# Dense products of a two-block float32 network: one matmul with plain float32 operands in place of three float32r passes

## The chip, the cores and the metric

The kernel runs on one core of a Trainium2 chip. The metric is the device time of one execution in microseconds (us). PE is the matrix engine (TensorE); a matmul holds one operand still in the array (the weights in PE's sense, loaded by LDWEIGHTS, here called PEld) and streams the columns of the other through it. DVE (VectorE), ACT (ScalarE) and POOL (GpSimd) work on elements; SP issues the transfers (DMA) from the chip's memory.

## What is computed

The input is x, 256 tokens of 1024 float32 features. Three parts follow one another; the dense products in them are what this case is about.

```python
# first block
p = rmsnorm(x) @ w_in                      # [256,1024] @ [1024,9248]
y_rnn = rglru_branch(...) @ w_rnn_proj     # [256,1536] @ [1536,1024]
y_dn = deltanet_branch(...) @ w_dn_proj    # [256,1024] @ [1024,1024]
x = x + (g_rnn * y_rnn + g_dn * y_dn) @ w_out
x = x + (silu(gt) * up) @ w_down           # gt, up = split(rmsnorm(x) @ w_gate_up)
# then two layers of: four attention-like branches from one wide projection,
# their gated sum through a projection, a layer norm, and a mixture of 16384 experts:
# a = gelu(x @ u.T); out = (gates * a) @ v   # u, v: [16384, 1024]
```

The program computes the expert part densely: the activations of all 16384 experts, times gates that are zero for those not chosen, times `v`. Everything is float32 from end to end.

## The kernel before

**Operands.** Every dense product is done in float32r, a form of float32 with fewer bits. To keep the accuracy of float32, each operand is cut into two float32r parts, `hi` (the value rounded) and `lo` (what is left), and a product is three passes into the same PSUM tile: hi x hi, lo x hi, hi x lo.

- `split_w` (L84) streams one block of weights, 128 rows of up to 1024 words (512 KB): SP issues the load of `wraw` (L91), ACT casts it to `whi` (L98; DVE in turns set by `share`), DVE subtracts and writes `wlo` (L100; POOL for two blocks). `wraw`, `whi` and `wlo` have three buffers each. `hold` can tie a block's two steps to come after given instructions, to keep them out of a norm's way.
- `split_x` (L108) does the same for an activation in SBUF: ACT writes `hi` (L111), DVE `lo` (L112).
- The normalized activations live as two tiles `xh` and `xl` of [128, 8, 256], written by `norm_evac` (L225) from PSUM: affine steps on ACT (L233) and DVE (L232), a copy for `hi` (L244), a subtraction for `lo` (L247).

**Products with stationary weights.** `lin_s` (L124) makes 128 output features for all 256 tokens from one block of weights of eight chunks: the 128x128 pieces of the block stand in the array and x^T streams, 256 columns at a time. For each chunk there is a pass with `whi` (L137) and one with `wlo` (L138) against `xh`, and after them eight passes of `whi` against `xl` (L140): 24 passes a block, into one bank `st` of two that alternate. Its `evac` takes the result out of PSUM.

**Products with moving weights.** `lin_m` (L144) keeps a 128x128 piece of x^T and streams the weights, 512 columns at a time, into four PSUM banks (two halves of the tokens, two of the columns). Per block these are four groups of three passes:

```python
mm(o, xh[:, kc, s], hi[:, c], start=first and n == 0, stop=False)   # L155
mm(o, xh[:, kc, s], lo[:, c], start=False, stop=False)              # L156
mm(o, xl[:, kc, s], hi[:, c], start=False, stop=last and n == len(steps) - 1)  # L157
```

In `mixers` the helper `project` does its products of 256 columns with `mm3` (L114, passes at L116 to L118).

**Order.** `block1` (L706), `mixers` (L1346) and `peer` (L1636) write out the order by hand. Chains of small work on DVE and ACT (a delta rule, a recurrence, attention, the routing of experts) are woven with blocks of `lin_s` by lists of calls (`units`, `weave`, `Fill`), so that PE always has a block to work on. All loads go through SP's queue in the order of the program, and a load waits there until its buffer is free.

`peer` is the longest part, and runs twice. Its 128 blocks of `u` go through `lin_s`: 50 of them (`X1`) while the routing runs, the others between 32 groups of `gates` (L1674), which build the gates of eight tokens with 16 products of f16 operands each (L1684, L1685). Then 128 blocks of `v` go through `lin_m`; for each the activations of 128 experts, `W[e // H][:, e % H]`, are split (`split`, L1657) one step ahead.

**Plain float32.** Many small products are plain float32 already: the normalizing transposes of `norm_T` (L222), the sums with alpha x in `add_alpha_x` (L78; it first adds `xh` and `xl` on DVE, L75), the recurrence's gates (L675), the delta rule's matrices (L473, L547, L636), the experts' keys (L1536).

Of the kernel before, what the change touches and what calls it, by code (L numbers as in the profile page):

```python
# [10 lines left out]
F32R = mybir.dt.float32r  # L11
# [9 lines left out]
P = 128  # L21
T = 256
# [5 lines left out]
ALPHA = 4.0 ** 0.25  # L28


class K:
    """Shared state of the program under construction and its small building blocks."""

    def __init__(self, ctx, tc, A):
        self.tc, self.nc, self.A = tc, tc.nc, A
        self.ctx = ctx
        E = ctx.enter_context
        self.cp = E(tc.tile_pool(name="cp", bufs=1))
        self.wp = E(tc.tile_pool(name="wp", bufs=4))
# [3 lines left out]
        self.held = []  # L43
        self.share(0)
# [35 lines left out]
    def share(self, *turns):  # L80
        """Engines of the first parts of the next weights: 1 for DVE, 0 for ACT, in turns."""
        self.turns = cycle(turns)

    def split_w(self, src, words, eng=None):  # L84
        """Stream one unit of weights and split it exactly into two float32r parts."""
        nc = self.nc
        self.hi_dve = next(self.turns)
        raw = self.t(self.wp, [P, 1024], "wraw", bufs=3)
        hi = self.t(self.wp, [P, 1024], "whi", F32R, bufs=3)
        lo = self.t(self.wp, [P, 1024], "wlo", F32R, bufs=3)  # L90
        nc.sync.dma_start(raw[:, :words], src)  # L91
        h = self.held.pop(0) if self.held else None
        after = lambda i: self.tc.issue_after(h[i].ins) if h and h[i] else nullcontext()
        with after(0):
            if self.hi_dve:
                nc.vector.tensor_copy(hi[:, :words], raw[:, :words])
            else:
                nc.scalar.copy(hi[:, :words], raw[:, :words])  # L98
        with after(1):
            (eng or nc.vector).tensor_sub(lo[:, :words], raw[:, :words], hi[:, :words].bitcast(F32))  # L100
        return hi, lo

    def hold(self, *after):
        """Keep the next splits of weights but the first out of the way of a norm: their two parts come after the given
        instructions."""
        self.held = [None, *after]

    def split_x(self, hi, lo, src):  # L108
        """hi + lo = src exactly; src in SBUF."""
        nc = self.nc  # L110
        nc.scalar.copy(hi, src)  # L111
        return nc.vector.tensor_sub(lo, src, hi.bitcast(F32))  # L112

    def mm3(self, out, lh, ll, rh, rl, start, stop):  # L114
        mm = self.nc.tensor.matmul
        mm(out, lh, rh, start=start, stop=False)  # L116
        mm(out, lh, rl, start=False, stop=False)
        mm(out, ll, rh, start=False, stop=stop)  # L118

    def units(self, x, src, evac, n, eng=None):  # L120
        """The products of lin_s as a list of calls."""
        return [lambda j=j: self.lin_s(x, src[j:j + 1], lambda _, o: evac(j, o), n=1, eng=eng) for j in range(n)]

    def lin_s(self, x, src, evac, kcs=(KC,), n=None, eng=None):  # L124
        """out^T tiles of 128 columns: weights stationary, x^T moving. src [units, 128, words]."""
        xh, xl = x
        u = 0
        for j in range(n):
            o = self.bank("st")
            c0, ct = 0, sum(kcs)  # L130
            for kc in kcs:
                hi, lo = self.split_w(src[u], kc * P, eng)
                u += 1
                mm = self.nc.tensor.matmul
# [9 lines left out]
    def lin_m(self, acc, steps, ncol, first, last):  # L144
        """token-layout out [t, col] += x^T[kc] w[kc] for steps (x, kc, source of w), by halves of t; acc[half][bank]."""
        ws = [self.split_w(src, ncol) for _, _, src in steps]
        mm = self.nc.tensor.matmul
        for h in range(2):
            s = slice(h * P, (h + 1) * P)
            for b in range((ncol + 511) // 512):  # L150
                c = slice(b * 512, min(ncol, (b + 1) * 512))
                o = acc[h][b][:, :c.stop - c.start]
                for n, ((xh, xl), kc, _) in enumerate(steps):
                    hi, lo = ws[n]
                    mm(o, xh[:, kc, s], hi[:, c], start=first and n == 0, stop=False)  # L155
                    mm(o, xh[:, kc, s], lo[:, c], start=False, stop=False)  # L156
                    mm(o, xl[:, kc, s], hi[:, c], start=False, stop=last and n == len(steps) - 1)  # L157

    def lin_m_all(self, acc, x, src, ncol, count, extra=None):
        """All chunks of a token-layout product, the last two together."""  # L160
# [9 lines left out]
    def rstd(self, out, ss, scale, eps):  # L170
        """out = (ss * scale + eps) ** -0.5 for few columns."""
# [6 lines left out]
    def softplus(self, out, y, pool, sign=1.0):  # L178
        """out = softplus(sign * y), accurate in relative terms, for few columns."""
# [17 lines left out]
    def transposes(self, y, kcs, evac):  # L197
        """PE-transposes of y [128 t, 2, f] (token layout) as a list of calls; evac(c, psum [128, 2, 256])."""
# [11 lines left out]
    def norm_T(self, pool, half, evac):  # L210
        """Transposes of a normalized x: half(h) -> y [128 t, 1024] and a scale [128 t, 1];
        evac(c -> psum [128, 256] of a chunk)."""
        nc = self.nc
        os = None
        for h in range(2):
            y, r = half(h)
            d = self.t(pool, [P, P], "nd", bufs=2)
            self.scaled = nc.vector.tensor_scalar(d, self.ident, r, None, op0=OP.mult)
# [6 lines left out]
    def norm_evac(self, pool, g, b, xx):  # L225
        """Gain, bias and exact split of transposed chunks."""
        nc = self.nc

        def affine(dst, o, c, eng):
            gs, bs = g[:, c:c + 1], b[:, c:c + 1] if b is not None else 0.0  # L230
            if eng:
                return nc.vector.tensor_scalar(dst, o(c), gs, bs, op0=OP.mult, op1=OP.add)  # L232
            return nc.scalar.activation(dst, o(c), AF.Identity, scale=gs, bias=bs)  # L233
# [17 lines left out]
    def rmsnorm_T(self, half, g, pool, xh, xl):  # L251
        """hi/lo of (rmsnorm(x) * g)^T; half(h) -> x [128 t, 1024] of a half, g [128, 8] per feature."""
# [10 lines left out]
        self.norm_T(pool, norm, self.norm_evac(pool, g, None, (xh, xl)))  # L263
# [23 lines left out]
def conv_tile(k, pads, n, o, w, dst, bias=None):  # L287
    """Centred 4-tap depthwise convolution along t of psum o [128, 256]; w [128, 4]."""
# [8 lines left out]
def weave(gen, units, per=1):  # L297
    """Run a generator with calls of a list between its steps."""
# [11 lines left out]
class Fill:  # L310
    """Calls to put where other work waits: fill(n) makes the next n, fill.upto(n) all before the n-th."""
# [26 lines left out]
class DeltaNet:  # L338
    """Gated delta rule of 8 heads in both directions, chunks of 128 tokens."""
# [13 lines left out]
    def project(self):  # L353
        """Keys and queries (unnormalized) and the gates' inputs."""
# [28 lines left out]
    def gates(self):  # L383
# [20 lines left out]
        # in the order (direction, head group, half, head), and its negative  # L404
# [41 lines left out]
    def matrices(self, hg):  # L446
        """Decayed k k^T (without the learning rates) and k q^T of 4 heads; both directions share a tile by triangles."""
# [32 lines left out]
    def small(self):  # L480
        """Inverses of the 32-blocks on the diagonal, scaled by the learning rates of their rows, and their transposes:
# [1316 lines left out]
```

## Time and profile before

| | us |
|---|---|
| median of 3 runs | 3051.55 (3049.89 to 3051.58) |
| span of the profiled execution, first to last instruction | 3042.9 |
| between the two | 8.65 |

The page gives no time of its own for the profiled execution beside its span; the difference to the median is what lies around the span in an execution. A profile lists for each instruction when it began and how long it was busy. For PE the beginnings are recorded and the ends are modelled, so consecutive records overlap in the list, and the distance from one beginning to the next is the time that an instruction really took from the engine. "float32r" and plain float32 operands both show as f32 in PE's rows; the line of the code tells them apart. The chain of waits follows the last instruction back to what released it, step by step.

### The profile page before, as it was taken

The page shows a single profiled execution, that of the slowest core. Times are in us where ns is not written, and L with a number is a line of the kernel's source. Part 1 is how long each engine was busy: PE and PEld are TensorE (multiplying, and loading weights), DVE is VectorE, ACT ScalarE, POOL GpSimd, SP SyncE. Part 2 cuts the span into 40 slices and gives each one's busy share as a digit, 9 for nine tenths or more (in the row PEclk, how much of TensorE's full clock was granted, in tenths as well). Part 3 has the DMA queues.
Part 4 walks back from the last instruction along what each step waited for, and adds up shares of the span by engine and source line. Part 5 has one row for each costly group of instructions (what it writes and reads, how often), then busy time and mean ns, then how long its engine had stood idle before and what let it go on. Part 6 is the DMA issues. An engine that isn't in the chain of part 4 may idle for free.

```text
span 3042.9 us, 50388 instructions
## 1 busy us (share of the span) xinstructions
PE 2977.5 (98%) x19954; PEld 2682.9 (88%) x19954; DVE 1990.7 (65%) x3464; ACT 1457.4 (48%) x2514; POOL 76.9 (3%) x96
## 2 busy tenths in 40 slices
PE   8989999999999999999999999999999999999998
PEld 7888999989999898888888889999989888888887
DVE  7787765565767965566556666576895565656565
ACT  6667644455444543333444446544453333344444
POOL 0012000000000000000000000000000000000000
PEclk9999999999999998888999999999998888899999
DMA  5342456553445443323455555345543323355554
GB/s 196 105 132 87 153 198 193 190 178 120 142 158 188 166 154 111 111 104 113 157 190 191 193 191 203 111 139 184 180 166 133 111 104 111 109 182 194 190 191 159
DMA packets 129742, 470.96 MB, mean 155 GB/s; under 512 B 14785, under 2 KB 15073, under 8 KB 128609
## 3 DMA queue, kind: packets, MB, share of 16 engines
q1 hardware_dynamic: 129504, 467.73, 45.1%
q8 instruction: 157, 2.57, 0.3%
q14 instruction: 81, 0.66, 0.1%
HBM read 466.63 MB, written 1.05 MB: 154 GB/s over the span
## 4 chain that ended last, share of the span: by engine, by line
PE 89%; DVE 6%; ACT 3%; issue 1%; POOL 1%; DMA 0%; SPq 0%; POOLq 0%; DVEq 0%; ACTq 0%
PE st L137 16%; PE st L138 15%; PE st L140 14%; PE acc L155 8%; PE acc L157 8%; PE acc L156 8%; PE bank L1684 4%; PE bank L1685 4%; DVE wlo L100 2%; PE bank L157 1%; PE bank L155 1%; PE bank L156 1%; PE bank L1290 1%; ACT whi L98 0%; PE bank L1536 0%
## 5 line engine op out<-in xcount | busy, mean ns | idle before, releaser
L100 DVE TENSOR_TENSOR wlo<-wraw,whi 128x1024 fp32r<-128x1024 f32 (+2 forms) x859 | 1048.0, 1222 | 424.7 <-ACT whi L98 421.6
L137 PE MATMUL st<-xh,whi 128*128 128x256 f32 x4040 | 1049.1, 297 | 8.4 <-ACT gy L784 2.2
L138 PE MATMUL st<-xh,wlo 128*128 128x256 f32 x4040 | 1022.1, 291 | 18.3 <-DVE wlo L100 18.3
L98 ACT CAST whi<-wraw 128x1024 fp32r<-128x1024 f32 (+2 forms) x852 | 887.2, 1042 | 183.4 <-PE st L140 51.8
L137 PEld LDWEIGHTS st<-xh,whi 128*128 128x128 f32 x4040 | 815.2, 202 | 32.6 <-issue 9.1
L138 PEld LDWEIGHTS st<-xh,wlo 128*128 128x128 f32 x4040 | 813.5, 201 | 26.5 <-DVE wlo L100 22.3
L140 PE MATMUL st<-xl,whi 128*128 128x256 f32 x4040 | 552.4, 280 | 0.2
L140 PEld LDWEIGHTS st<-xl,whi 128*128 128x128 f32 x4040 | 506.8, 190 | 2.0 <-DVE xl L247 1.0
L155 PE MATMUL acc<-whi,wwh 128*128 128x512 f32 x1024 | 404.8, 395 | 0.0
L157 PE MATMUL acc<-whi,wwl 128*128 128x512 f32 x1024 | 401.6, 392 | 0.0
L156 PE MATMUL acc<-wlo,wwh 128*128 128x512 f32 x1024 | 397.7, 388 | 0.0
L111 ACT CAST wwh<-W 128x256 fp32r<-128x256 f32 x256 | 104.0, 407 | 363.6 <-PE acc L156 357.5
L157 PEld LDWEIGHTS acc<-whi,wwl 128*128 128x128 f32 x1024 | 192.3, 188 | 45.0
L156 PEld LDWEIGHTS acc<-wlo,wwh 128*128 128x128 f32 x1024 | 192.3, 188 | 42.4
L155 PEld LDWEIGHTS acc<-whi,wwh 128*128 128x128 f32 x1024 | 192.6, 188 | 37.8
L1684 PE MATMUL bank<-oah,ob 128*128 128x128 f16 x512 | 212.9, 416 | 0.1
L1685 PE MATMUL bank<-oal,ob 128*128 128x128 f16 x512 | 211.4, 413 | 0.0
L112 DVE TENSOR_TENSOR wwl<-W,wwh 128x256 fp32r<-128x256 f32 x256 | 108.6, 425 | 151.9 <-ACT wwh L111 149.7
L1691 DVE SCALAR_TENSOR_TENSOR W<-bank,W 128x512 f32<-128x512 f32 (+26 forms) x114 | 59.4, 557 | 194.2 <-PE bank L1685 194.2
L1702 ACT ACTIVATE ge<-st 128x8 f32<-128x8 f32 (+25 forms) x156 | 44.4, 284 | 291.9 <-PE st L140 291.9
L1694 ACT ACTIVATE W<-bank 128x96 f32<-128x96 f32 (+16 forms) x76 | 29.4, 404 | 203.2 <-DVE W L1691 203.2
L1685 PEld LDWEIGHTS <-ob 128*128 128x128 f16 x512 | 75.9, 148 | 39.5
(518 smaller groups left out, 2957.1 us busy)
## 6 DMA issues: line engine op xcount, KB each, us to landing
wraw<-in_u SPq DMA_DIRECT2D x256, 512.0 KB, 3.3
wraw<-in_v SPq DMA_DIRECT2D x256, 512.0 KB, 3.3
wraw<-in_w SPq DMA_DIRECT2D x173, 512.0 KB, 3.5
wraw<-in_wg SPq DMA_DIRECT2D x44, 512.0 KB, 4.3
wraw<-in_wq SPq DMA_DIRECT2D x32, 512.0 KB, 3.3
wraw<-in_wo SPq DMA_DIRECT2D x24, 512.0 KB, 4.2
wraw<-in_wdn SPq DMA_DIRECT2D x22, 512.0 KB, 4.3
wraw<-in_wb SPq DMA_DIRECT2D x16, 512.0 KB, 3.5
```

Source lines behind the costliest of these rows:

```text
L98: nc.scalar.copy(hi[:, :words], raw[:, :words])
L100: (eng or nc.vector).tensor_sub(lo[:, :words], raw[:, :words], hi[:, :words].bitcast(F32))
L111: nc.scalar.copy(hi, src)
L112: return nc.vector.tensor_sub(lo, src, hi.bitcast(F32))
L137: mm(o[:, :T], hi[:, s], xh[:, c0 + c], start=c0 + c == 0, stop=False)
L138: mm(o[:, :T], lo[:, s], xh[:, c0 + c], start=False, stop=False)
L140: mm(o[:, :T], hi[:, c * P:(c + 1) * P], xl[:, c0 + c], start=False, stop=c0 + c == ct - 1)
L155: mm(o, xh[:, kc, s], hi[:, c], start=first and n == 0, stop=False)
L156: mm(o, xh[:, kc, s], lo[:, c], start=False, stop=False)
L157: mm(o, xl[:, kc, s], hi[:, c], start=False, stop=last and n == len(steps) - 1)
L1684: nc.tensor.matmul(b[:, i], bb[:, :, i], ah[:, :, i], start=True, stop=False)
L1685: nc.tensor.matmul(b[:, i], bb[:, :, i], al[:, :, i], start=False, stop=True)
```

## The change

The split goes, on both sides of every dense product. `load_w` loads a block into one of ten buffers and nothing else; `xx`, `yy`, `dd`, `mm`, `br` and the hidden activations are single float32 tiles, written once; `lin_s`, `lin_m` and `project` issue one matmul per product, in the same order of blocks as before, with `start` and `stop` moved to the first and last of them. `share`, `hold`, `split_w`, `split_x` and `mm3` are dropped, and with them the two blocks whose subtraction POOL did. `peer` reads the activations of the experts straight from `W`. A few steps of `block1` around the removed halves are written differently: the factor 0.5 moves into `hdn` and into one more ACT multiplication in `rnn`. Comments were removed throughout, so lines move.

```diff
+WB = 10
...
-    def add_alpha_x(self, acc, xx, c, pool):
-        f = self.t(pool, [P, T], "ax", bufs=2)
-        self.nc.vector.tensor_add(f, xx[0][:, c].bitcast(F32), xx[1][:, c].bitcast(F32))
+    def add_alpha_x(self, acc, xx, c):
         for h in range(2):
             o = acc[h][c // 4][:, (c % 4) * P:(c % 4 + 1) * P]
-            self.nc.tensor.matmul(o, f[:, h * P:(h + 1) * P], self.ai, start=False, stop=False)
...
-    def split_w(self, src, words, eng=None):
...
+            self.nc.tensor.matmul(o, xx[:, c, h * P:(h + 1) * P], self.ai, start=False, stop=False)
+
+    def load_w(self, src, words):
+
+        w = self.t(self.wp, [P, 1024], "w", bufs=WB)
+        self.nc.sync.dma_start(w[:, :words], src)
+        return w
...
             for kc in kcs:
-                hi, lo = self.split_w(src[u], kc * P, eng)
+                w = self.load_w(src[u], kc * P)
                 u += 1
-                mm = self.nc.tensor.matmul
                 for c in range(kc):
-                    s = slice(c * P, (c + 1) * P)
-                    mm(o[:, :T], hi[:, s], xh[:, c0 + c], start=c0 + c == 0, stop=False)
-                    mm(o[:, :T], lo[:, s], xh[:, c0 + c], start=False, stop=False)
-                for c in range(kc):
-                    mm(o[:, :T], hi[:, c * P:(c + 1) * P], xl[:, c0 + c], start=False, stop=c0 + c == ct - 1)
+                    self.nc.tensor.matmul(o[:, :T], w[:, c * P:(c + 1) * P], x[:, c0 + c], start=c0 + c == 0,
+                                          stop=c0 + c == ct - 1)
...
-                for n, ((xh, xl), kc, _) in enumerate(steps):
-                    hi, lo = ws[n]
-                    mm(o, xh[:, kc, s], hi[:, c], start=first and n == 0, stop=False)
-                    mm(o, xh[:, kc, s], lo[:, c], start=False, stop=False)
-                    mm(o, xl[:, kc, s], hi[:, c], start=False, stop=last and n == len(steps) - 1)
+                for n, (x, kc, _) in enumerate(steps):
+                    self.nc.tensor.matmul(o, x[:, kc, s], ws[n][:, c], start=first and n == 0,
+                                          stop=last and n == len(steps) - 1)
...
         def ev(o):
-            fs = []
-            for c in (0, 1):
-                affine(xx[0][:, c], o, c, c)
-            for c in (2, 4, 6, 0):
-                f = self.t(pool, [P, 2, T], "nf", bufs=4)
-                for i in range(2):
-                    a = affine(f[:, i], o, c + i, 0)
-                if c:
-                    nc.vector.tensor_copy(xx[0][:, c:c + 2], f)
-                fs.append((c, f))
-            for c, f in fs:
-                v = nc.vector.tensor_sub(xx[1][:, c:c + 2], f, xx[0][:, c:c + 2].bitcast(F32))
-            self.hold((None, self.scaled), (a, v))
+            for c in range(KC):
+                gs, bs = g[:, c:c + 1], b[:, c:c + 1] if b is not None else 0.0
+                if c % 2:
+                    nc.vector.tensor_scalar(xx[:, c], o(c), gs, bs, op0=OP.mult, op1=OP.add)
+                else:
+                    nc.scalar.activation(xx[:, c], o(c), AF.Identity, scale=gs, bias=bs)
...
-            ws = [first]
-            for e in range(P - 2):
-                ws.append(split(e + 1))
-                k.lin_m(acc, [(ws[e], 0, A["v2"][n][e])], D, e == 0, False)
-                if e % 2 and e < 16:
-                    k.add_alpha_x(acc, xx, e // 2, p)
-            ws.append(split(P - 1))
-            k.lin_m(acc, [(ws[e], 0, A["v2"][n][e]) for e in (P - 2, P - 1)], D, False, True)
+        step = lambda e: (W[e // H], e % H, A["v2"][n][e])
+        for e in range(P - 2):
+            k.lin_m(acc, [step(e)], D, e == 0, False)
+            if e % 2 and e < 16:
+                k.add_alpha_x(acc, xx, e // 2)
+        k.lin_m(acc, [step(P - 2), step(P - 1)], D, False, True)
```

## Rows read from the trace of the kernel before

**Rows 1.** the page's span, and each engine's busy us, share of the span, instructions

```profile
span 3042.9 us, 50388 instructions
...
PE 2977.5 (98%) x19954; PEld 2682.9 (88%) x19954; DVE 1990.7 (65%) x3464; ACT 1457.4 (48%) x2514; POOL 76.9 (3%) x96
```

**Rows 2.** the chain of waits, its shares of the span by line

```profile
by line: PE st L137 15.9%; PE st L138 15.5%; PE st L140 14.5%; PE acc L155 8.3%; PE acc L157 8.3%; PE acc L156 8.1%; PE bank L1684 4.0%; PE bank L1685 3.9%; DVE wlo L100 1.9%; PE bank L157 1.2%; PE bank L155 1.2%; PE bank L156 1.2%; issue 0
```

**Rows 3.** timeline of PE, one block of `lin_s` (start us, us, what)

```profile
1002.04 0.28 PE L137 MATMUL st<-xh,whi 128*128 128x256 f32 x1
...
1003.86 1.07 PE L140 MATMUL st<-xl,whi 128*128 128x256 f32 x8
1004.76 0.28 PE L137 MATMUL st<-xh,whi 128*128 128x256 f32 x1
```

**Rows 4.** timeline of PE in `lin_m`, 18 passes from first to last

```profile
1539.67 0.39 PE L156 MATMUL acc<-wlo,wwh 128*128 128x512 f32 x1
...
1543.79 0.39 PE L156 MATMUL acc<-wlo,wwh 128*128 128x512 f32 x1
```

**Rows 5.** PE by form: count, then busy us, mean ns, idle before

```profile
L137 PE MATMUL st<-xh,whi 128*128 128x256 f32 x4040 | 1049.1, 297 | 8.4 <-ACT gy L784 2.2 <-DVE qk L1392 1.9 <-DVE xh L232 1.6
...
L155 PE MATMUL acc<-whi,wwh 128*128 128x512 f32 x1024 | 404.8, 395 | 0.0
...
L155 PE MATMUL bank<-whi,mh 128*128 128x512 f32 x96 | 38.8, 404 | 0.0
...
L116 PE MATMUL st<-brh,whi 128*128 128x256 f32 x128 | 36.7, 287 | 1.3 <-DVE mg L1367 1.3
...
L155 PE MATMUL acc<-whi,fah 128*128 128x512 f32 x88 | 34.7, 395 | 0.0
...
L137 PE MATMUL st<-yh,whi 128*128 128x256 f32 x96 | 24.1, 287 | 0.0
...
L137 PE MATMUL st<-dh,whi 128*128 128x256 f32 x64 | 15.7, 285 | 0.0
...
L155 PE MATMUL bank<-whi,xh 128*128 128x512 f32 x32 | 12.7, 396 | 0.0
...
L155 PE MATMUL bank<-whi,xh 128*128 128x412 f32 x32 | 11.2, 351 | 0.0
...
L78 PE MATMUL acc<-ai,ax 128*128 128x128 f32 x64 | 9.7, 274 | 0.0
```

**Rows 6.** the chain of waits in order of time, two runs of plain products

```profile
112.76 1.12 PE bank L473 x2
...
273.56 1.73 PE acc L675 x8
```

**Rows 7.** lengths of single records, L675 and L473 (min/median/max ns)

```profile
L675 PE MATMUL acc<-uT,rg_w x96: 378/379/483, 150.1 to 314.1; 128*128 128x256 f32 x96
...
L473 PE MATMUL bank<-gm,cst x16: 592/592/697, 110.3 to 142.7; 128*128 128x512 f32 x16
```

**Rows 8.** the page's line of the split, and PE's wait for it

```profile
L100 DVE TENSOR_TENSOR wlo<-wraw,whi 128x1024 fp32r<-128x1024 f32 (+2 forms) x859 | 1048.0, 1222 | 424.7 <-ACT whi L98 421.6
...
L98 ACT CAST whi<-wraw 128x1024 fp32r<-128x1024 f32 (+2 forms) x852 | 887.2, 1042 | 183.4 <-PE st L140 51.8
...
PE st L138 <- DVE wlo L100: 18.3, 19, 2.0
```

**Rows 9.** DMA: queue (packets, MB, share), and one load of weights

```profile
q1 hardware_dynamic: 129504, 467.73, 45.1%
...
wraw<-in_u SPq DMA_DIRECT2D x256, 512.0 KB, 3.3
```

**Rows 10.** the chain of waits at the start

```profile
3.61 7.57 DMA wraw<-in_w
```

**Rows 11.** engines by stretch: length, busy (x) by engine, granted clock, DMA

```profile
238.00:244.20 6.20, 6.10 (x51) 5.94 (x52) 4.44 (x6) 4.08 (x8) 2.08 (x4) 1.00 0.27 89
1137.40:1140.80 3.40, 3.40 (x18) 3.13 (x17) 2.33 (x4) 0.71 (x2) 0.00 (x0) 0.50 0.13 48
```

More of the change, by code (lines that the diff above doesn't have):

```diff
@@ L84, in split_w @@
-    def split_w(self, src, words, eng=None):
[L86 to L114, printed above, removed]
-        mm = self.nc.tensor.matmul
[L116 to L122, printed above, removed]
@@ L124, in lin_s, with units @@
-    def lin_s(self, x, src, evac, kcs=(KC,), n=None, eng=None):
-        xh, xl = x
+            self.nc.tensor.matmul(o, xx[:, c, h * P:(h + 1) * P], self.ai, start=False, stop=False)
[3 more added lines that the diff above has]
+        return w
+    def units(self, x, src, evac, n):
+        return [lambda j=j: self.lin_s(x, src[j:j + 1], lambda _, o: evac(j, o), n=1) for j in range(n)]
+    def lin_s(self, x, src, evac, kcs=(KC,), n=None):
@@ L144, in lin_m @@
     def lin_m(self, acc, steps, ncol, first, last):
-        ws = [self.split_w(src, ncol) for _, _, src in steps]
-        mm = self.nc.tensor.matmul
+        ws = [self.load_w(src, ncol) for _, _, src in steps]
         for h in range(2):
@@ L223, in norm_T, with norm_evac, rmsnorm_T @@
         evac(lambda c: os[c // 2][:, c % 2 * T:(c % 2 + 1) * T])
-    def norm_evac(self, pool, g, b, xx):
+    def norm_evac(self, g, b, xx):
         nc = self.nc
[L229 to L233, printed above, removed]
-        def ev(o):
-            fs = []
-            for c in (0, 1):
-                affine(xx[0][:, c], o, c, c)
-            for c in (2, 4, 6, 0):
-                f = self.t(pool, [P, 2, T], "nf", bufs=4)
-                for i in range(2):
-                    a = affine(f[:, i], o, c + i, 0)
-                if c:
-                    nc.vector.tensor_copy(xx[0][:, c:c + 2], f)
-                fs.append((c, f))
-            for c, f in fs:
-                v = nc.vector.tensor_sub(xx[1][:, c:c + 2], f, xx[0][:, c:c + 2].bitcast(F32))
-            self.hold((None, self.scaled), (a, v))
+        def ev(o):
+            for c in range(KC):
[4 more added lines that the diff above has]
+                    nc.scalar.activation(xx[:, c], o(c), AF.Identity, scale=gs, bias=bs)
         return ev
-    def rmsnorm_T(self, half, g, pool, xh, xl):
+    def rmsnorm_T(self, half, g, pool, xx):
         nc = self.nc
@@ L262, in norm @@
             return x, r
-        self.norm_T(pool, norm, self.norm_evac(pool, g, None, (xh, xl)))
+        self.norm_T(pool, norm, self.norm_evac(g, None, xx))
 V1 = dict(mix=8, ffn=8, dnw=96, rgw=48, rgb=12, ba=24, bx=24, lam=24, dnn=1, dtb=16, alog=16)
@@ L784, in ev_y, with ev @@
                     nc.scalar.activation(g, o, AF.Gelu_apprx_tanh)
-                    nc.vector.tensor_mul(g, g, uT[:, j])
-                    ys.append(k.split_x(yy[0][:, j], yy[1][:, j], g))
+                    ys.append(nc.vector.tensor_mul(yy[:, j], g, uT[:, j]))
                 ys = []
                 us = k.units(xx, A["w1"][37:49], ev_y, 12)
-                k.share(1)
-                for u in us[:4]:
-                    u()
-                k.share(0)
-                run(us[4:])
+                run(us)
                 mixT = uT[:, :8]
                 def rnn(j):
-                    k.lin_s(yy, A["wr1"][2 * j:2 * j + 2], lambda _, o: nc.vector.scalar_tensor_tensor(
-                        mixT[:, j], gates[j], 1.0, o, op0=OP.add, op1=OP.mult), kcs=(6, 6), n=1)
+                    def ev(_, o):
+                        y = k.t(yp, [P, T], "dp", bufs=2)
+                        nc.vector.scalar_tensor_tensor(y, gates[j], 1.0, o, op0=OP.add, op1=OP.mult)
+                        nc.scalar.mul(mixT[:, j], y, 0.5)
+                    k.lin_s(yy, A["wr1"][2 * j:2 * j + 2], ev, kcs=(6, 6), n=1)
                 for j in range(4):
@@ L836, in half @@
                     return x[:, h]
-                k.rmsnorm_T(half, V["ffn"], yp, *xx)
+                k.rmsnorm_T(half, V["ffn"], yp, xx)
         with k.pool("ffn") as fp, k.banks(2, 4):
@@ L955, in half @@
         return y, r
-    k.norm_T(pool, half, k.norm_evac(pool, gcol, bcol, xx))
+    k.norm_T(pool, half, k.norm_evac(gcol, bcol, xx))
 def layernorm_out(k, pool, src, gb, out):
@@ L1016, in norm @@
         return y, r
-    k.norm_T(pool, norm, k.norm_evac(pool, gcol, bcol, xx))
+    k.norm_T(pool, norm, k.norm_evac(gcol, bcol, xx))
 V2 = dict(l1g=8, l1b=8, l2g=8, l2b=8, gng=2, gnb=2, glg=2, gab=1, pos=32)
@@ L1364, in project @@
                         s = slice(c * 512 + (j % 4 + i) * P, c * 512 + (j % 4 + i + 1) * P)
-                        k.mm3(b[:, i * T:(i + 1) * T], hi[:, s], lo[:, s], br[0][:, q, c], br[1][:, q, c], c == 0, c == 1)
+                        nc.tensor.matmul(b[:, i * T:(i + 1) * T], w[:, s], br[:, q, c], start=c == 0, stop=c == 1)
                 g, y = gates[:, 8 * q + j:8 * q + j + 2], gates[:, j:j + 2]
@@ L1436, in mixers @@
         with k.pool("mx", 1) as mp:
-            mm += [k.t(mp, [P, KC, T], "mh", F32R), k.t(mp, [P, KC, T], "ml", F32R)]
+            mm.append(k.t(mp, [P, KC, T], "mm"))
             fill.upto(len(fill.units))
             acc = k.acc4()
-            k.lin_m_all(acc, mm, A["wo2"][n], D, KC, lambda c: k.add_alpha_x(acc, xx, c, mp))
+            k.lin_m_all(acc, mm[0], A["wo2"][n], D, KC, lambda c: k.add_alpha_x(acc, xx, c))
             layernorm(k, mp, acc, V["l1g"], V["l1b"], xx)
@@ L1646, in u_tile @@
         def u_tile(e, out):
-            k.lin_s(xx, A["u2"][n][e:e + 1], lambda _, o: nc.scalar.activation(out, o, AF.Gelu), n=1,
-                    eng=nc.gpsimd if e in (29, 32) else None)
+            k.lin_s(xx, A["u2"][n][e:e + 1], lambda _, o: nc.scalar.activation(out, o, AF.Gelu), n=1)
         us = iter(range(X1))
@@ L1655, in fill @@
                 break
-        def split(e):
-            ww = k.t(wp1, [P, 1, T], "wwh", F32R, bufs=2), k.t(wp1, [P, 1, T], "wwl", F32R, bufs=2)
-            k.split_x(ww[0][:, 0], ww[1][:, 0], W[e // H][:, e % H])
-            return ww
         with k.banks(6, 0):
@@ L1713, in peer @@
                         done += 1
-                first = split(0)
                 for e in range(done, P):
```

48 lines of the change are left out of this document (15 added, 33 removed).

## The prediction, made before the changed kernel was run

> **What bounds the kernel now.** The page's first table comes first, because one engine may already fill the span. The reader is to see that PE is busy for 98% of 3042.9 us, DVE for 65% and ACT for 48% [rows 1]. A busy PE is not yet a bound, so the chain of waits is read next: the dense products alone (L137, L138 and L140 in `lin_s`, L155 to L157 in `lin_m`) are 74% of the span. Of the two steps that split the weights only one has weight on the chain, `wlo` with 1.9%, which is 58 us [rows 2]. So the kernel stands or falls with what PE pays for one dense product, and the question of this change is a price: three float32r passes against one matmul with plain float32 operands.
>
> **The old price.** The timeline shows it best, since the ends of matmuls are modelled and only starts can be trusted. In `lin_s` the next block of eight products begins 2.72 us after the last, 24 passes of 0.1133 us each [rows 3]. In `lin_m` 18 passes of 512 columns take from 1539.67 to 1543.79, 0.229 us each [rows 4]. The counts come from the groups by form [rows 5]; the other two passes of a product have the same counts as the one shown. There are 4040 + 96 + 64 = 4200 products of 256 columns in `lin_s`, 1024 + 96 + 88 + 32 = 1240 of 512 columns and 32 of 412 in `lin_m`, and 128 of 256 in `project`. On PE they cost 4200 x 3 x 0.1133 = 1428 us, 1240 x 3 x 0.229 = 852, 32 x 3 x 0.184 (412/512 of the pass) = 18, and 128 x 3 x 0.1133 = 44. Together 2341 us.
>
> **The new price.** The kernel already has plain float32 matmuls, and they show two things. First, each is issued as two records: `add_alpha_x` makes 32 products per kind of PSUM tile, and its group counts 64 [rows 5]. Second, a record takes about twice the time per column. Eight records of L675 with 256 columns take 1.73 us of the chain, 0.216 us each [rows 6], where a float32r pass of the same width takes 0.113. So one plain product of 256 columns costs 2 x 0.216 = 0.432 us and the three passes that it replaces 0.340 us: **the single matmul is 27% dearer than the three.** A long run of plain records with 512 columns isn't in the trace. What it has are the lengths of single records, by their medians 379 ns for 256 columns (L675) and 592 for 512 (L473) [rows 7]: 213 ns for 256 more columns, so 0.216 + 0.213 = 0.429 us a record and 0.858 a product. The upper end is L473 itself, two records in 1.12 us of the chain [rows 6], or 1.12 us a product. The lower end is two records at a float32r pass's 0.229, 0.458 a product; that is rival 1. I take 0.858, because L473 runs as one product alone after a wait, while `lin_m` runs four in a row, like L675's eight records.
>
> The new sum: 4200 x 0.432 = 1814 us, 1240 x 0.858 = 1064, 32 x 0.69 = 22, 128 x 0.432 = 55. Together 2956 us. The change on PE is **+615 us**.
>
> A rule that would give another sign must be set against this. The row shows 0.216 us for one record and 0.432 for a product. The Trainium skill, Perfetto Trace Analysis, section Engine Utilization, gives TensorE's peak as 307.2 G output elements a second and halves it for FP32_LOW_HIGH. Read as the rate of a whole product, that is an estimate of 0.213 us for 128 x 256 outputs, and the sum would fall to about 2115 us in place of 3608. The trace agrees with the halving for one record and not for the product, which is two of them.
>
> **What goes away.** The splits (859 DVE subtractions of 1222 ns, 852 ACT casts of 1042 ns [rows 8]), those of the activations, the second halves in `norm_evac`, the DVE additions in `add_alpha_x`: about half of the work of both engines. Nearly all of it lies beside PE. It is worth what stands on the chain, 58 us for `wlo` [rows 2]; the casts aren't among the lines that the chain lists, and I count them at nothing. Ends: 0, if another wait takes over each time, and 58 plus the rest of PE's idle time, 65 us [rows 1], of which at most some 47 (65 less the 18 that the waits put down to `wlo` [rows 8]) are not `wlo`'s. I take 58, because a block now holds PE for 8 x 0.432 = 3.46 us instead of 2.72, so every producer has more time. What would be late next is the weights' DMA: 3.3 us to landing against 3.46 us of PE a block, with ten buffers in place of three; the queue's packets fill 45.1% of the old span, about 1372 us [rows 9]. I count it at nothing; without the ten buffers each block would risk some tenths of a us.
>
> **What is added or moved.** PE now waits for the DMA itself, and SP's queue for PE's release of a buffer ten blocks back; behind it wait the small loads (gate weights, constants, `x`), now issued up to ten blocks ahead. At the start ten loads of 512 KB go out instead of three. The first load of weights takes 7.57 us there [rows 10]. If all that are out shared the engines evenly, ten for three, it would take 25, so 18 us more; if they finish in the order of issue, nothing. I take nothing, the end nearer to 3.3 us to landing, which every later load keeps with two more behind it [rows 9]. In `norm_evac` four ACT and four DVE operations write `xx` straight; a chunk is read every 0.43 us, and the norms' waits for `nd` stay. `rnn` gets an ACT multiplication for each of eight tiles, under 2 x 3.46 us of PE: nothing. The gelu, gates and routing chains keep their operations and lose DVE neighbours.
>
> The clock: plain float32 alone keeps it, as the stretch from 238.0 to 244.2 us has nothing but such matmuls and is granted 1.00; pieces at 1.2 GHz come after the f16 gate products of L1684 and L1685, as at 1137.4, where 0.50 was granted [rows 11]. Those products stay, sixteen in a row, so I leave that loss as it is.
>
> **Sum.** 3042.9 + 615 - 58 = 3600 us of span. The median of the runs is 8.65 us above the span of the profiled execution, which I add unchanged: **3608 us**, 18% slower.
>
> **Rivals.**
> 1. *A plain product costs one record's time* (its two records run at the pace of a float32r pass, or a single one is issued for these lines). Then the dense work is 2341 x 2/3 = 1561 us, and the time 3051.6 - 780 - 58 = 2214 us, still above the DMA's 1372. It decides below 0.170 us a record (half of 0.340): faster under it, slower over it. For it speaks the rule above; against it L675, 0.216 us, and the doubled counts [rows 5, 6]. Chance 0.03.
> 2. *The clock falls under long plain streams.* At 0.50 every dense record takes up to twice its time, so 2956 us more: about 6560 us. For it speaks that no plain run in the trace is longer than a few us; against it the 1.00 of the stretch at 238 us [rows 11]. Chance 0.03.
> 3. *Wide plain products cost what L473 shows.* 1240 x (1.12 - 0.858) = 325 us more, 3933 us; with half of it, 3770. Against it speaks that the doubling per column holds for 128 and 256 columns alike. Chance 0.04.
>
> **How the numbers follow.** The forecast keeps 0.90. Low end: 3608 - 47 (PE's other idle time) = 3561. High end: nothing saved (+58), 18 us at the start and 5 ns more on each of the 2480 wide records (12 us) give 3696. I put the range at 3560 to 3695; it leaves out the three rivals and a little of the forecast. About 0.2% is what a measurement of this kernel can tell from no change. Faster has rival 1's 0.03; slower has all else, 0.97; no case ends between.
>
> **What would show it.** Right: per dense product two PE records, 8400 from `lin_s` and about 2540 from `lin_m`; 16 records of a block 3.46 us from block to block; four wide products in 3.43 us; PE at 99% of the span, DVE and ACT near a third; no `wlo` on the chain; a granted clock below 1.00 for long only in the two stages of gate products. Wrong: a block under 2.72 us, dense stretches at 0.50, wide records over 0.45 us, or DMA on the chain.

## The result, and the profile after

The changed kernel takes 3540.01 us (3539.66 to 3542.02, 4 runs), 489 us more than the kernel before on the same chip (3050.78 us); the ratio is 1.161, with an interval of 1.160 to 1.163. The prediction had the side and the price of a plain product right and the size 68 us too high: 3540 lies 20 us under the low end of its range.

The span and the engines of the changed kernel, to be read against [rows 1]:

```profile
span 3538.1 us, 35236 instructions
...
PE 3501.9 (99%) x14354; PEld 2519.3 (71%) x14354; DVE 821.1 (23%) x2213; ACT 525.4 (15%) x1338; POOL 62.0 (2%) x92
```

DVE has lost 1170 us of work and ACT 932, and nothing of that shows in the time: PE was the bound before and is so more than before. What PE does is seen in the groups by form (count, then busy us and mean ns of one) of the changed kernel; L96 is the one matmul of `lin_s`, L110 that of `lin_m`, L1296 that of `project`:

```profile
L96 PE MATMUL st<-xx,w 128*128 128x256 f32 x8080 | 1819.5, 384 | 12.0 <-DVE zT L676 4.9 <-ACT W L1575 4.4 <-DVE mg L1298 1.9
L110 PE MATMUL acc<-w,W 128*128 128x512 f32 x2048 | 881.9, 592 | 0.0
...
L1296 PE MATMUL st<-br,w 128*128 128x256 f32 x256 | 57.3, 381 | 0.0
```

8080 records where [rows 5] has 4040 products of this kind: two to a product. From the timeline of PE, first 32 records of L96 between two runs of gate products, then seven of L110 up to a product of another line:

```profile
1319.12 7.09 PE L96 MATMUL st<-xx,w 128*128 128x256 f32 x32
1326.05 0.39 PE L1606 MATMUL bank<-oah,ob 128*128 128x128 f16 x1
...
1699.15 3.17 PE L110 MATMUL acc<-w,W 128*128 128x512 f32 x7
...
1702.16 0.61 PE L74 MATMUL acc<-ai,xx 128*128 128x128 f32 x4
```

From 1319.12 to 1326.05 are 6.93 us, 0.2166 us a record; from 1699.15 to 1702.16 are 3.01 us, 0.430 a record. Before, three passes took 0.340 us [rows 3] and 0.687 [rows 4]; now a product takes 0.433 and 0.860.

The granted clock is where the two differ in a way that was not forecast. The two stages that hold the gate products, of the kernel before (start and end, length, busy us and count of PE, PEld, DVE, ACT and POOL, granted clock, then DMA):

```profile
1105.00:1462.00 357.00, 356.95 (x2263) 314.41 (x2262) 212.63 (x332) 116.21 (x259) 0.00 (x0) 0.87 0.31 108
2306.00:2668.00 362.00, 361.95 (x2270) 319.35 (x2269) 213.39 (x333) 116.10 (x259) 0.00 (x0) 0.86 0.31 107
```

and of the changed kernel:

```profile
1281.00:1667.00 386.00, 386.00 (x1687) 307.68 (x1686) 129.34 (x257) 47.38 (x184) 0.00 (x0) 0.96 0.33 100
2688.00:3074.00 386.00, 386.00 (x1687) 307.34 (x1686) 129.03 (x256) 47.50 (x185) 0.00 (x0) 0.96 0.32 100
```

The gate products are the same in both, 64 runs of sixteen f16 matmuls. But before, the mean clock of these stages is 0.87 and 0.86, after it 0.96. With levels of 1 and one half, that is 2 x 0.13 x 357 + 2 x 0.14 x 362 = 194 us at 1.2 GHz before and 2 x 0.04 x 772 = 62 us after. These go by rounded shares; the trace's own record of the clock has 191 and 55 us.

The weights' queue, and the longest waits of PE in the changed kernel (us in total, times, longest):

```profile
q1 hardware_dynamic: 129504, 467.73, 42.1%
...
w<-in_u SPq DMA_DIRECT2D x256, 512.0 KB, 3.6
```

```profile
PE bank L176 <- DVE nd L172: 14.2, 7, 8.0
PE st L96 <- DVE zT L676: 4.9, 4, 1.7
```

A load lands in 3.6 us. No wait for a split is left; the norms' waits for `nd` (L172 now, L218 before) stay.

### The profile page after: what moved, and what is told of

It reads as the page before. It is cut to its first block, busy times and chain, and to the rows that moved or that the text cites. A ratio compares the mean times of both kernels' runs of the same rounds, so it can differ in the third digit from the quotient of the medians.

```text
span 3538.1 us, 35236 instructions
## 1 busy us (share of the span) xinstructions
PE 3501.9 (99%) x14354; PEld 2519.3 (71%) x14354; DVE 821.1 (23%) x2213; ACT 525.4 (15%) x1338; POOL 62.0 (2%) x92
## 4 chain that ended last, share of the span: by engine, by line
PE 76%; issue 6%; DVE 3%; POOL 0%; ACT 0%; DVEq 0%; POOLq 0%; ACTq 0%
PE st L96 37%; PE acc L110 25%; PE bank L1606 3%; PE bank L1607 3%; PE bank L110 3%; PE st L1296 1%; PE bank L1221 1%; PE bank L1464 0%; DVE bi L1433 0%; DVE cand L1431 0%; DVE bi L1430 0%; PE bank L74 0%; PE acc L74 0%; PE bank L176 0%; DVE bs L1429 0%
## 5 line engine op out<-in xcount | busy, mean ns | idle before, releaser
L96 PE MATMUL st<-xx,w 128*128 128x256 f32 x8080 | 1819.5, 384 | 12.0 <-DVE zT L676 4.9
L96 PEld LDWEIGHTS st<-xx,w 128*128 128x128 f32 x8080 | 1546.3, 193 | 256.3 <-issue 22.9
L110 PE MATMUL acc<-w,W 128*128 128x512 f32 x2048 | 881.9, 592 | 0.0
L110 PEld LDWEIGHTS acc<-w,W 128*128 128x128 f32 x2048 | 387.9, 190 | 481.3 <-issue 470.2
L1627 DVE TENSOR_TENSOR W<-W,ge 128x8 f32<-128x8 f32 (+25 forms) x156 | 46.9, 301 | 340.8 <-ACT ge L1624 340.8
L1607 PEld LDWEIGHTS <-ob 128*128 128x128 f16 x512 | 74.5, 146 | 44.4
L1606 PEld LDWEIGHTS <-ob 128*128 128x128 f16 x512 | 74.4, 145 | 40.1 <-DVE oah L1603 0.5
L110 PE MATMUL bank<-w,mm 128*128 128x512 f32 x192 | 84.9, 592 | 0.0
L110 PE MATMUL acc<-w,fa 128*128 128x512 f32 x176 | 78.8, 592 | 0.0
L1575 ACT ACTIVATE W<-st 128x256 f32<-128x256 f32 x100 | 38.4, 384 | 263.4 <-PE st L96 263.4
L110 PEld LDWEIGHTS bank<-w,mm 128*128 128x128 f32 x192 | 35.6, 190 | 38.9 <-issue 38.0
L110 PEld LDWEIGHTS acc<-w,fa 128*128 128x128 f32 x176 | 33.4, 190 | 33.6 <-issue 32.3
```

The source lines that it names most:

```text
L96: self.nc.tensor.matmul(o[:, :T], w[:, c * P:(c + 1) * P], x[:, c0 + c], start=c0 + c == 0, stop=c0 + c == ct - 1)
L110: self.nc.tensor.matmul(o, x[:, kc, s], ws[n][:, c], start=first and n == 0, stop=last and n == len(steps) - 1)
L1575: k.lin_s(xx, A["u2"][n][e:e + 1], lambda _, o: nc.scalar.activation(out, o, AF.Gelu), n=1)
L1606: nc.tensor.matmul(b[:, i], bb[:, :, i], ah[:, :, i], start=True, stop=False)
L1607: nc.tensor.matmul(b[:, i], bb[:, :, i], al[:, :, i], start=False, stop=True)
L1627: nc.vector.tensor_mul(w[:, :td], w[:, :td], ge[:, :td])
```

## Experiments

The theory after the result, **clock**: the price of a product is as forecast, and what is missing from the 557 us of the forecast (615 - 58) is time that the change wins back at 1.2 GHz after the runs of gate products. Its rival, **stalls**: the waits on the splits were worth far more than 58 us. Each figure is a median, set against the kernel before as it ran on the same chip, where it took 3043.5 to 3047.2 us. The changed kernel's 3540 is from another chip, so differences to it are good to some 4 us.

**1 and 2. Break up the runs of gate products, in both kernels.**

```diff
                     for i in range(8):
+                        if i == 4 and mid:
+                            u_late(done, t0)
+                            done += 1
                         nc.tensor.matmul(b[:, i], bb[:, :, i], ah[:, :, i], start=True, stop=False)
...
-                    gates(8 * i, done)
+                    gates(8 * i, done, i > 0)
+                    done += i > 0
```

> The kernel before, with one block of u moved into the middle of each group of gate products, so that the sixteen f16 products stand as eight, a block, eight. The same work. Theory clock (the change won back pieces at 1.2 GHz that follow the runs of sixteen): the granted clock stays at 1.00 in the two gate stages, and the time falls by about 80 us, to some 2970 us. Theory stalls (the change won back more waits on the splits than the 58 us of the forecast, the clock is a side show): the time stays within 15 us of 3051.

> The changed kernel with the same move of one block. Theory clock: 17 pieces at half clock are left to lose, so about 28 us less, some 3512 us; the difference to the kernel before with broken runs is then 540 to 560 us, as the forecast's sum 615 - 58 had it, and not the 489 us measured between the two unbroken kernels. Theory stalls: the difference stays at about 490 us.

Measured: 2973.15 us against 3046.72 (ratio 0.976, 0.974 to 0.978), so 74 us less; and 3514.16 us, 26 us less than the 3540 of the unbroken changed kernel. The clock of the first gate stage in experiment 1, and in 2:

```profile
1111.00:1438.00 327.00, 326.95 (x2303) 286.08 (x2301) 213.33 (x336) 118.27 (x264) 0.00 (x0) 1.00 0.37 120
```

```profile
1283.00:1660.00 377.00, 377.00 (x1707) 303.70 (x1706) 130.09 (x260) 47.86 (x187) 0.00 (x0) 1.00 0.35 104
```

Both are at 1.00, with the same matmuls on PE as the unbroken kernels. In the four gate stages of the two runs two pieces at 1.2 GHz are left, each behind the first group of a second stage, which the edit leaves whole (`i > 0`). The difference between the two kernels with the clock nearly out of play is 541 us, at the lower edge of what the theory clock gave, and not 490. So about 74 - 26 = 48 of the missing 68 us are the clock. The theory stalls falls as the main cause.

**3 and 4. No low part of the weights,** without and with broken runs.

```diff
-        lo = self.t(self.wp, [P, 1024], "wlo", F32R, bufs=3)
...
-        with after(1):
-            (eng or nc.vector).tensor_sub(lo[:, :words], raw[:, :words], hi[:, :words].bitcast(F32))
-        return hi, lo
+        return hi, hi
```

> The kernel before without the DVE subtraction that makes the low part of the weights; the passes that used it read the high part instead, so the low part of the weights is left out of the products. PE's work is the same 16800 passes. By the chain of waits 58 us go, so about 2993 us, if the clock in the gate stages does as before; theory stalls wants 110 us or more, under 2940 us.

> The same without the low part of the weights, and with the gate runs broken up, so that the clock plays no part. Against the kernel before with broken runs: theory clock expects 58 us less (the term of the forecast, measured with the clock out of play), some 2910 us; theory stalls expects 110 us less or more.

Measured: 3023.32 us against 3046.72, and 2946.11 against the 2973.15 of experiment 1: 23 and 27 us less. Both theories missed. The subtraction of the weights is worth half of what its 1.9% of the chain [rows 2] says. Of PE's waits in experiment 4 (L219 is `norm_T`, L134 the first pass of `lin_s`, W the activations of the experts) the two longest are

```profile
PE bank L219 <- DVE nd L215: 13.5, 7, 8.1
PE st L134 <- ACT W L1644: 7.9, 4, 3.3
```

and `wlo`'s 18.3 us [rows 8] are gone; others have grown a little. PE's idle time, 67 us of the span in experiment 1, is 47 us in experiment 4. A share of the chain names the work that ended last, not what would be saved without it.

**5 and 6. Move the runs of gate products apart.** If the clock is what differs, why did it differ, with the same runs? Experiment 5 makes the float32r blocks between the runs longer (below); 6 does so with the plain ones, by one more product with zeros in a block.

```diff
                 for c in range(kc):
                     s = slice(c * P, (c + 1) * P)
                     mm(o[:, :T], hi[:, s], xh[:, c0 + c], start=c0 + c == 0, stop=False)
                     mm(o[:, :T], lo[:, s], xh[:, c0 + c], start=False, stop=False)
+                for c in range(more):
+                    mm(o[:, :T], lo[:, c * P:(c + 1) * P], xl[:, c0 + c], start=False, stop=False)
```

> The kernel before with four more float32r passes (low part by low part) in each of the 156 blocks of u that stand between the groups of gate products: 28 passes a block instead of 24, 3.17 us instead of 2.72, and 71 us more of PE work. Theory spacing (how often a run of gate products is followed by a piece at 1.2 GHz hangs on the distance from run to run, not on the kind of operands beside it): some 16 to 20 pieces instead of 55 in the two stages, and the time hardly moves, 3040 to 3065 us. Theory operands (plain float32 beside the gate products holds the clock better than float32r does): as many pieces as before, and 71 us more, about 3120 us.

> The changed kernel with one more plain product (by zeros) in each of the same 156 blocks: nine instead of eight, 3.89 us instead of 3.46, 67 us more of PE work. Theory spacing: 40 to 48 pieces instead of 17, so 67 plus some 45 us, about 3650 us. Theory operands: 17 pieces as before, and 67 us more, about 3607 us.

Measured: 3056.7 us against 3046.62, ten more, for 71 us of added PE work; and 3657.67 us, 118 more than 3540, for 67 us of added work. The clock of the first gate stage in 5 and in 6:

```profile
1115.00:1475.00 360.00, 359.95 (x2566) 317.07 (x2565) 211.48 (x332) 116.62 (x260) 0.00 (x0) 0.98 0.33 107
```

```profile
1283.00:1726.00 443.00, 443.00 (x1827) 353.15 (x1826) 129.11 (x256) 47.33 (x184) 0.00 (x0) 0.90 0.29 87
```

0.98 where it was 0.87, with float32r beside the gates; 0.90 where it was 0.96, with plain operands. In the two stages the trace has 11 pieces at the lower level in experiment 5 (56 in the kernel before) and 49 in experiment 6 (16 in the changed kernel). So it is not the kind of operand that holds the clock. The same runs are followed by a piece at 1.2 GHz more or less often with the distance from one to the next, and the change, by making a block 3.46 us long for 2.72, happened on a better distance. What makes a distance good is not shown: with blocks of 2.72, 3.17, 3.46 and 3.89 us there are 56, 11, 16 and 49 pieces, so longer is not always better. Nor was it tested whether the zeros in experiment 6 play a part.

**7. One part of the change alone:** plain operands for the experts' output weights only.

```diff
+    def lin_m1(self, acc, steps, ncol, first, last):
...
+                    self.nc.tensor.matmul(o, x[:, kc, s], ws[n][:, c], start=first and n == 0,
+                                          stop=last and n == len(steps) - 1)
...
-                k.lin_m(acc, [(ws[e], 0, A["v2"][n][e])], D, e == 0, False)
+                k.lin_m1(acc, [step(e)], D, e == 0, False)
```

> One part of the change alone, on the kernel before: only the products with the experts' output weights (1024 of the 1240 wide ones) take plain float32 operands, in three buffers; all else keeps its three passes. If a wide plain product costs 0.858 us for 0.687, that is 175 us more, about 3226 us, since that stage has no gate products and few waits. If the narrow price doesn't carry over to 512 columns (two records in 1.12 us), 440 us more, about 3490.

Measured: 3222.23 us against 3046.62 (ratio 1.058, 1.056 to 1.060), 175.6 us more. Its wide plain products, by form:

```profile
L172 PE MATMUL acc<-wraw,W 128*128 128x512 f32 x2048 | 882.2, 592 | 0.5 <-DMA wraw<-in_v 0.5
```

The price of the wide product, which the trace of before could only bound, is met: 175 us were expected. That it agrees to the microsecond is chance, as the runs spread from 3214 to 3228 us, but the 440 us of the other case are far off, in a stage where neither clock nor waits blur the price.

**8. Three buffers instead of ten.**

```diff
-WB = 10
+WB = 3
```

> The changed kernel with three buffers of weights instead of ten. If two loads ahead are enough (a block is 3.46 us of PE, a load 3.6 us to landing), the time stays within 10 us of 3540. If the ten buffers hide the loads, as the prediction had it, some tenths of a us per block on 876 blocks, 90 us or more.

Measured: 3540.70 us (3539.73 to 3543.33). The ten buffers do nothing; the prediction's remark that they hide tenths of a us a block was wrong, though no term of the sum hung on it.

**9 and 10. What else was won?** With the clock out of play 541 us are left of the 615 that PE's price makes: 74 us saved, of which the low part of the weights is 27. A first guess for the rest was the first float32r pass after a matmul of another kind. Plain products of 16 columns of zeros were put between the wide ones of the last stage, in both kernels with broken runs (the cut is from the kernel before).

```diff
+                    if nil:
+                        mm(o[:, :16], self.ident, self.sel[:, :16], start=False, stop=False)
                     mm(o, xl[:, kc, s], hi[:, c], start=False, stop=last and n == len(steps) - 1)
```

> The kernel before with broken runs, and in the stage of the experts' output weights one plain float32 product of 16 columns of zeros between the float32r passes of each group, 1008 in all. Theory switch (a float32r pass that follows a matmul of another kind starts its successor 0.1 to 0.2 us late, which the changed kernel no longer pays): the added products cost 0.1 to 0.2 us more each than the same products cost beside plain operands (next run), so 100 to 200 us more in all. Theory none (a switch is free, and what the change won besides the clock and the low parts is waits on casts and norms): the same cost as in the next run, within 30 us.

> The changed kernel with broken runs, with the same 1008 plain products of 16 columns of zeros. Two records of a narrow product take some 0.06 us each (records of 15 columns in the trace of before), so 0.12 us a product, about 120 us over 3514, 3635 us. Both theories agree here; this run is the measure for the one before.

Measured: 3216.27 us, 243 over experiment 1, and 3739.05, 225 over experiment 2: 18 us apart on 1008 products. The guess falls for wide passes. In the traces of experiments 1 and 2 it has little room with narrow ones either: at the some 300 places where dense work follows another matmul, the two records around the change take 9 us more in all with float32r. Timelines of PE, float32r (L158 is the added product) and plain (L113):

```profile
1640.02 0.40 PE L156 MATMUL acc<-wlo,wwh 128*128 128x512 f32 x1
1640.26 0.29 PE L158 MATMUL acc<-sel,ident 128*128 128x16 f32 x2
1640.40 0.47 PE L159 MATMUL acc<-whi,wwl 128*128 128x512 f32 x1
1640.71 0.40 PE L155 MATMUL acc<-whi,wwh 128*128 128x512 f32 x1
```

```profile
1800.86 0.29 PE L113 MATMUL acc<-sel,ident 128*128 128x16 f32 x2
1801.00 1.10 PE L110 MATMUL acc<-w,W 128*128 128x512 f32 x2
1801.94 0.29 PE L113 MATMUL acc<-sel,ident 128*128 128x16 f32 x2
```

The pass after the added product takes 0.31 us until the next starts, 0.08 over its usual 0.23; and the two records of the plain product take 0.94, 0.08 over 0.86. It is the narrow product that costs its successor this, whatever kind that is. Also, an added product costs 0.22 us in the plain kernel, not the 0.12 expected.

**11. The operands of the gate products side by side.**

```diff
-                    al, ah, bb = (k.t(p, [P, P, 8], m, F16) for m in ("oal", "oah", "ob"))
-                    c = [r[:, None, t0:t0 + 8] for r in rt]
+                    al, ah, bb = (k.t(p, [P, 8, P], m, F16) for m in ("oal", "oah", "ob"))
+                    c = [r[:, t0:t0 + 8, None] for r in rt]
...
-                        nc.tensor.matmul(b[:, i], bb[:, :, i], ah[:, :, i], start=True, stop=False)
+                        nc.tensor.matmul(b[:, i], bb[:, i], ah[:, i], start=True, stop=False)
```

> The kernel before with broken runs, and the operands of the gate products laid out so that the 128 numbers that PE reads stand next to one another in a partition (before, every eighth). If the 0.232 us of such a pass come from that stride, 1024 passes fall to some 0.06 us each, 176 us less than 2973, about 2800 us; the four DVE operations that build the operands may lose speed by it, from 0.68 to 1.1 us each at the least good, 108 us of DVE in stages of 940 us, which would give some of that back. If the stride isn't the cause, 2973 or somewhat more.

Measured: 2874.29 us against 3043.5 (ratio 0.944, 0.942 to 0.946), 99 us under experiment 1. It is the fastest version here. Two gate products of the kernel before, ten apart on PE's timeline, and one of its four DVE steps:

```profile
1134.93 0.42 PE L1684 MATMUL bank<-oah,ob 128*128 128x128 f16 x1
...
1137.25 0.42 PE L1684 MATMUL bank<-oah,ob 128*128 128x128 f16 x1
```

```profile
L1680 DVE TENSOR_TENSOR ob<-io,rt 128x1024 f16<-128x1024 f16 x64 | 43.7, 683 | 0.0
```

Three consecutive gate products now:

```profile
1205.15 0.22 PE L1687 MATMUL bank<-oah,ob 128*128 128x128 f16 x1
1205.21 0.22 PE L1688 MATMUL bank<-oal,ob 128*128 128x128 f16 x1
1205.26 0.22 PE L1687 MATMUL bank<-oah,ob 128*128 128x128 f16 x1
```

A product takes 0.056 us in place of 0.232. Not all of the 180 us arrive, since DVE pays for the layout, as the line of the same step and the first gate stage show:

```profile
L1680 DVE TENSOR_TENSOR ob<-io,rt 128x1024 f16<-128x1024 f16 x64 | 78.3, 1224 | 0.0
...
1105.00:1379.00 274.00, 254.82 (x2266) 242.23 (x2265) 269.74 (x334) 115.81 (x258) 0.00 (x0) 0.98 0.44 140
```

1.22 us instead of 0.68 for each of the four steps, and DVE is now busy for 270 of 274 us: in this stage it has become the bound. Which of the two operands' layouts PE gains from was not separated.

**12. No low parts at all.** As experiment 4, and the activations' low parts gone too.

```diff
-        nc.scalar.copy(hi, src)
-        return nc.vector.tensor_sub(lo, src, hi.bitcast(F32))
+        return nc.scalar.copy(hi, src)
...
-        xh, xl = x
+        xh = xl = x[0]
```

> The kernel before with broken runs, without the low parts of the weights and of the activations (the passes read the high parts instead, so all low parts are left out), the norms' results written straight as in the changed kernel, and no addition ahead of the alpha x products. What is left of the splits is the ACT cast of the weights; PE has its three passes. Against the changed kernel with broken runs, 3514, the price alone would be 615 less, 2899 us. Theory waits (what the change won beyond the low parts of the weights lies in the activations' splits and the norms): 2900 to 2915 us. Theory passes (it lies in float32r passes that run a few ns longer than the best blocks from which the 2341 us were read, and in the first pass after another kind of matmul): 2935 to 2946, hardly less than without the weights' low parts alone.

Measured: 2942.30 us, 4 less than experiment 4. The theory waits falls: the activations' splits, the norms' longer ends and the additions before alpha x were hidden. 43 us (3514 - 2942 = 572 against 615) are left between the two. The size is what the theory passes expected, and the traces bear out one half of that theory, the passes that run longer than the best blocks. The prediction read its price from a block of 2.72 us; another of the kernel before, at a granted clock of 1.00 and with no wait, takes 2.82:

```profile
2673.59 0.28 PE L137 MATMUL st<-xh,whi 128*128 128x256 f32 x1
...
2676.41 0.28 PE L137 MATMUL st<-xh,whi 128*128 128x256 f32 x1
```

Over all float32r passes of 256 columns at full clock and without a wait, the starts lie 0.1149 us apart on average in the kernel before and 0.1145 in experiment 12, where the prediction put 0.1133. That is about 18 of the 43 us. The other half, the first pass after another kind, experiment 9 spoke against. The ACT cast of the weights is still in this kernel; PE's waits put down to it are 4.2 us, but a kernel without the cast alone was not tried.

## Why the prediction was right or wrong

**The price of a product** was right, and it is nearly the whole result. Records per product, 0.216 and 0.429 us, and 3.46 us a block were read from a few plain products of the kernel before, and the changed kernel shows 0.2166 and 0.430. The choice between 0.858 and the 1.12 us of the lone pair of L473 was right too (experiment 7: 175.6 us for 175). Rivals 1 and 3 are out. The price of the three passes was a little low: [rows 3] is one of the quickest blocks, and with the averages of the trace of before the old sum is some 22 us more than 2341, so the change on PE some 593 us for the forecast 615.

**The clock term was wrong, and it took the result out of the range.** The failing step is "Those products stay, sixteen in a row, so I leave that loss as it is." The products stayed, the loss did not. [rows 11] showed a piece at 0.50 after a run; I took it as a cost of the run, fixed with it, and gave it no bounds. The loss was 74 us before and 26 us after (experiments 1 and 2), because it hangs on when the runs come (experiments 5 and 6), and every block's length moved that. An honest bound would have been from nothing lost at all, 74 us less, to a piece after every run. With that low end the range would have held the result. On rival 2, plain operands in long streams do keep the clock: it is 1.00 in a stage of `lin_m` without gate products, and experiment 2 has it at 1.00 even among them.

```profile
1740.00:2120.00 380.00, 380.00 (x887) 168.31 (x886) 0.70 (x1) 0.00 (x0) 0.00 (x0) 1.00 0.51 159
```

**What goes away** was put at 58 us, all of it for the subtraction of the weights, and that was twice too much: the subtraction is worth 27 (experiment 4), the activations' low parts 4, which is within the spread of the runs (experiment 12), and PE's idle time fell by 29 us in all, from 65 to 36. That 615 less 541 leaves 74, near the 58, is luck: the 74 are a remainder, with some 20 us in it for the old price and an estimated 10 for the clock, since experiment 1 still runs 34 us at 1.2 GHz, mostly outside the gate stages, and experiment 2 runs 13. Zero for the casts was a guess that was never tested alone.

**The moved and added work** cost next to nothing: no wait for a load stands among PE's waits; the first block of `lin_s` starts 3 us later than before (16.1 us for 13.0), behind the norm's second half, which waits for DVE, not for the loads, and before it stood still after three passes until 16.0. That the ten buffers were needed was wrong (experiment 8).

In all: 615 for the products less 48 for the clock and 74 for the rest gives 493 for the measured 489, but that closes by itself, as the 74 are what was left. The records of the two unbroken traces, added up from start to start, account for the 495 us between their spans in another way: 615 at the forecast prices; 62 less in dense passes that run at 1.2 GHz (90 us lost there before, 28 after); 22 less because the float32r passes cost more than forecast; 27 less in waits before dense products; 9 less in the rest. So the clock is the largest part by either way, 48 or 62 us. That the experiments give the lower figure fits the 62 new places where dense work starts again in the broken runs, but this was not tested.

The 8.65 us between span and median, which the sum adds, are not what lies around a span: in every run whose own time is known the two are about 2 us apart (3539.83 and 3538.1 in the changed kernel). The profiled execution of the kernel before was about 7 us quicker than the median. The forecast, which starts from that same span, is not moved by it.

## What to carry to other kernels

One instruction in the source need not be one pass: count an operation's records in a trace and the distance between their starts before trading three of one kind for one of another. Read the old price from an average and not from one quick block. Work that an engine off the critical path is spared is worth only what it stands for in the waits; here its share of the chain said 58 us and its removal gave 27. A loss that comes after something, such as the lower clock after a run of gate products, belongs to the timing of the loop and not to the run alone: give it bounds when a change alters the loop's period, and try breaking the run up, which here is worth 74 us for a few lines.

## What was not expected of the hardware

By the profile PE is without a gap in the gate stages (busy for 356.95 of 357 us in the kernel before), and still the granted clock falls there: the gate products, 128 columns in 0.232 us, stand before 56 of the 62 falls in the trace. With the operands laid side by side, the same products take 0.056 us. And 71 us of added matmuls cost 10 us (experiment 5), because with the runs further apart most of the pieces at 1.2 GHz failed to come.
